# Moving blocks read as two halves in alternation, and PSUM read with a step of two, in a streaming-encoder layer

## The chip, the cores and the metric

The kernel runs on one core of one Trainium2 chip. Its metric is the device time of one execution in microseconds; the program is launched once and holds the whole layer. TensorE (PE) multiplies a stationary block of 128 columns, which it loads first (PEld), with a moving block of up to 512 columns and writes the products to PSUM. VectorE (DVE) and ScalarE (ACT) read PSUM; GpSimd (POOL) and SyncE (SP) start transfers.

## The reference, cut to what matters

```python
x = x + 0.5 * swiglu_ffn(rmsnorm(x, ffn1_norm), w_gate1, w_up1, w_down1)
x = x + hybrid_mixer(rmsnorm(x, mix_norm), w_in, q_norm, k_norm, rel_bias, pool_w, pool_scale, w_out)
x = x + 0.5 * swiglu_ffn(rmsnorm(x, ffn2_norm), w_gate2, w_up2, w_down2)
return rmsnorm(x, final_norm)

def swiglu_ffn(x, w_gate, w_up, w_down):
    return (silu(x @ w_gate) * (x @ w_up)) @ w_down
```

x has 512 tokens of 1024 features, the feed-forward width is 2816, all in float32. The mixer projects to q, k, v (512 columns each, 8 heads of 64) and u (512 columns). Attention is in chunks of 64 over the own and the 8 previous chunks, with normalised q and k and a learned bias. u goes through trailing means over 2, 4, 8 and 16 tokens, less the token itself, a 128x128 map and a scale for each of four groups. Both results, side by side, go through `w_out`.

## The kernel before, in words

**A product of high and low parts.** Each float32 operand is split in a high part (ScalarE's cast to float32r) and the remainder (VectorE). `mm3` makes one product of two such pairs as three matmuls into one PSUM bank: high x high (L188), high x low (L189), low x high (L190). Each matmul loads its own stationary block. Every large product of the kernel goes through `mm3`.

**The stages.** First comes the norm of x and the up stage of the first feed-forward layer (gate and up projections). The first feature blocks (5 in the first layer, 4 in the second, "plain") are multiplied as they are, with all 512 tokens as the moving block; meanwhile VectorE and ScalarE prepare sums and differences of token halves and feature halves (`blocks`). The other 17 and 18 blocks are multiplied in a scheme with seven products in place of eight: a unit for one block has 7 x 4 calls of `mm3` with moving blocks of 256 tokens. In a unit the order on PE, DVE and ACT is written out by hand. ScalarE copies some of the results out of PSUM (`copy`, L561) or takes their silu (L626), and VectorE adds others (L605, L619), multiplies gate and up (`place`, L717) and makes sums and remainders of the next unit's weights (L472, L490, L496, L497).

The down stage uses the same scheme of seven products (`Down`). The first layer has weights as the stationary and 256 tokens as the moving block; the second has tokens as the stationary and 512 (in part 256) weight columns as the moving block. `gain` and `shared` (first layer), `residual` and a list of additions (second) bring the results into x.

The mixer lies between the layers. Its steps are jobs with an engine, a cost and a rank, and `plan` puts them in order: it simulates the engines with these costs. The cost of one `mm3` is the constant `T_MM3`. Projections on PE fill in wherever nothing of higher rank is ready. The jobs' buffers and their places in PSUM come out of the same plan. Weight transfers of the mixer are jobs on SP (L1101), with a cast on ScalarE (L1106) and a remainder on VectorE (L1111). The norm's steps on TensorE are four products of one column with `ones` (L1140; L309 in the up stages) and a product of 512 columns in full float32 (L1171; L330 in the up stages). Transposes of q and k are at L1344. Scores, transposes of the probabilities and the products with v (L1501, L1565, L1590) call TensorE directly, without `mm3`.

**Where operands lie.** High and low parts of the weights lie in `parts_sb` at offsets that are given by hand, in the unit loop with a shift of 16 columns (`SHIFT`).

Of the kernel before, what the change touches and what calls it, by code (L numbers as in the profile page):

```python
# [12 lines left out]
ALU = mybir.AluOpType  # L13
# [34 lines left out]
)  # L48
HOP = 0.45
SLOW = dict(act=1.06, dve=1.06)  # L50
T_MM3 = 0.685
MIX_ENGINES = {
    mybir.EngineType.PE, mybir.EngineType.DVE, mybir.EngineType.Activation, mybir.EngineType.Pool,
}
# [2 lines left out]
def layer(  # L57
# [117 lines left out]
    def weights(src, parts=1):  # L175
# [6 lines left out]
            split(raw[:, part], hi[:, part], lo[:, part])  # L182
        return hi, lo

    def mm3(acc, a, b, start, stop, further=False):

        more = dict(skip_group_check=True) if further else {}
        nc.tensor.matmul(acc, a[0], b[0], start=start, stop=False, **more)  # L188
        nc.tensor.matmul(acc, a[0], b[1], start=False, stop=False, **more)  # L189
        nc.tensor.matmul(acc, a[1], b[0], start=False, stop=stop, **more)  # L190

    def cut(pair, lo, n):
        return pair[0][:, lo : lo + n], pair[1][:, lo : lo + n]
# [208 lines left out]
    def ffn_up(norm, wA, down, loaded, in_order, plain, turns=()):  # L402
# [8 lines left out]

        def evacuate(f, gate, up):
            g = temp()
            nc.vector.tensor_tensor(g, gate, norm.rb, op=ALU.mult)
            sg = temp()
            nc.scalar.activation(sg, g, AF.Silu)

            nc.vector.tensor_tensor(sg, sg, norm.rb, op=ALU.mult)
            down.place(f, up, sg)
            down.sums(f)  # L420
            return sg

# [135 lines left out]
                )  # L558

        def copy(dst, src, scale=1.0):  # L560
            nc.scalar.activation(dst, src, AF.Copy, scale=scale)  # L561

        def nothing():
            pass
# [4 lines left out]
        with tc.manual_schedule(engines={E.PE, E.DVE, E.Activation}):  # L569
            last_silu = last_place = last_sums = nothing  # L570
            for n in range(plain, KF):
                f = down.order[n]
                acc, up_lo, up_hi = bank()[:, :HT], bank()[:, :HT], abank()[:, :HT]
                u, z, sg = temp(), temp(), temp()
                w11, w13, w24 = (w[n, i][:2] for i in (11, 13, 24))
                if n == KF - 1:
                    down.load(new_sum())
                    down.load(new_sum())
                product(acc, w11, A11, True)
                ends = n == KF - 1  # L580
# [12 lines left out]
                low11(n + 1)  # L593
                if ends:
                    down.first_tokens(0)
                last_sums()
                sum13(n + 1)
                copy(z[:, HT:], up_hi, -1.0)
                product(acc, cut(w24, 0, S), S2, False)
                copy(u[:, HT:], acc, -1.0)  # L600
                sum24(n + 1)
                if ends:
                    down.first_tokens(1)
                product(up_hi, cut(w24, S, S), A22, False)
                nc.vector.tensor_tensor(u[:, HT:], up_hi, u[:, HT:], op=ALU.add)  # L605
                down.make_sums(u[:, HT:])
                if ends:
                    down.first_weights(0)
                product(acc, cut(w13, 0, S), S1, False)
                copy(z[:, :HT], acc)  # L610
                nc.vector.tensor_tensor(z[:, HT:], z[:, :HT], z[:, HT:], op=ALU.add)
# [7 lines left out]
                nc.vector.tensor_tensor(u[:, :HT], up_lo, u[:, :HT], op=ALU.add)  # L619
                low24(n + 1)  # L620
                if ends:
                    down.first_weights(1)
                product(acc, cut(w22, 0, S), S4, False)

                def last_silu(acc=acc, sg=sg):
                    nc.scalar.activation(sg[:, :HT], acc, AF.Silu, scale=-1.0)  # L626

                def last_place(f=f, u=u, sg=sg):
                    down.place(f, u, sg)
# [16 lines left out]
    class Down:  # L646
# [65 lines left out]
        def place(self, f, up, sg):  # L712
            k, second = self.pair(f)
            z = self.acts[k // 2][:, :, k % 2, :]
            up, sg = (y.rearrange("p (a c) -> p a c", a=2) for y in (up, sg))
            at = z[:, A12 : A22 + 1] if second else z[:, A11 : S3 + 1 : S3 - A11]
            nc.vector.tensor_tensor(at, up, sg, op=ALU.mult)  # L717

        def sums(self, f):

# [132 lines left out]
    with tc.tile_pool(name="act1", bufs=1, reuse_waits="tile") as apool, ExitStack() as in_order:  # L853
# [20 lines left out]

        def gain(i, d, t, acc, scale):
            z = whole_of(i, d, t)
            scaled(z, acc[i][0][0].rearrange("p (a c) -> p a c", a=2), scale, z)

        def shared(i, d, t, op):
            z = whole_of(i, d, t)  # L880
            nc.vector.tensor_tensor(z, z, u2[i].rearrange("p (a c) -> p a c", a=2), op=op)

        down1.product(p7, 0, S3, T3)
        for i in range(2):
# [45 lines left out]
    with tc.tile_pool(name="mix", bufs=1, reuse_waits="tile") as mpool:  # L930
# [366 lines left out]
        def project_qk(half, first):  # L1297
            var = {}

            def evacuate(t):  # L1300
                return lambda: nc.scalar.activation(
                    buf["q", half, t], buf[half, t], AF.Copy, scale=n2.r[:, t : t + 1]
                )

            def square(t):
# [74 lines left out]
        def project_v(first):  # L1380
            def finished(t, unit):
                def pair():
                    if v[t] is None:
                        v[t] = mpool.tile([P, NH, 2, HD], F32R, tag=f"v{t}", name=f"v{t}")
                    return v[t][:, :, 0, :], v[t][:, :, 1, :]

                high, low = scaled_pair(
                    lambda: buf["v", t].rearrange("p (h c) -> p h c", c=HD), pair,
                    lambda: n2.r[:, t : t + 1],
                )  # L1390
                z = job("act", 0.65, RANK["evac"], high, [unit, at_r])
# [6 lines left out]
        def project_u(g, first):  # L1398
# [8 lines left out]
            def evacuate():  # L1407
                u = buf["uu", g]
                nc.gpsimd.memset(u[:, :PAD], 0.0)
                nc.vector.tensor_tensor(u[:, PAD:], buf["u", g], n2.rb, op=ALU.mult)  # L1410

            def sums():
                s, step, n = buf["uu", g], 1, 0
# [33 lines left out]
            for k in range(KD):  # L1447
# [10 lines left out]
            z = job("dve", 0.62, rank, low, [z], uses=[("dd", g)])  # L1458
            z = job("pe", 0.71, RANK["map"], mapped, [z, at_wp], [("bank", ("map", g))], pair)
            high, low = scaled_pair(  # L1460
                lambda: buf["map", g], lambda: (buf["pT", g, 0], buf["pT", g, 1]),
                lambda: ps_sb[:, g : g + 1],
            )
            z = job("act", 0.65, rank, high, [z], [("m", ("pT", g, n)) for n in range(2)])
# [187 lines left out]

        def add_out(d):
            def emit():
                nc.vector.tensor_tensor(x[d], x[d], buf["out", d], op=ALU.add)

            return emit

# [90 lines left out]
    with tc.tile_pool(name="act2", bufs=1, reuse_waits="tile") as apool, ExitStack() as in_order:  # L1749
# [21 lines left out]
        def residual(half, t, acc, lo=0, n=S, scale=0.5):  # L1771

            z = xt[half * NT + t][:, lo : lo + n]
            nc.vector.scalar_tensor_tensor(z, acc[:, :n], scale, z, op0=ALU.mult, op1=ALU.add)

        def settle(half, t, part, lo=0, n=S):

# [56 lines left out]
        for tt in range(2):  # L1834
            scaled(u2[tt], p1[tt][0][0], 0.5, u2[tt], ALU.subtract)
            residual(1, 2 + tt, p5[tt][0][0])
            for i in (2 + tt, NT + tt, NT + 2 + tt):
                op = ALU.subtract if i < NT + 2 else ALU.add
                todo.append((nc.vector.tensor_tensor, xt[i], xt[i], u2[tt], op))
        for g in range(G):  # L1840
            if g + 1 < G:
                down2.product(p7, g + 1, S3, T3)
# [154 lines left out]
```

## Time and profile before

| what | value |
|---|---|
| time, median of 3 runs | 830.56 us (830.5 to 831.28) |
| span of the profiled execution, first to last instruction | 828.4 us |
| DVE busy in the span | 713.3 us, 86% |
| ACT busy | 500.3 us, 60% |
| POOL busy | 147.2 us, 18% |
| moved by DMA | 158.56 MB, 191 GB/s on average |

The profiled execution has no time of its own beside its span; the median of the runs stands 2.2 us above that span. [...] In lists of groups, `x8 | 3.3, 417` means eight instructions, 3.3 us busy in all, 417 ns each. On the line of a window the numbers with counts are the busy times of PE, PEld, DVE, ACT and POOL in this order, then the granted clock, the share of the DMA engines and GB/s.

### The profile page before, as it was taken

What the parts mean: (1) busy time and instruction counts of PE and PEld (TensorE: products, weight loads), DVE (VectorE), ACT (ScalarE), POOL (GpSimd) and SP (SyncE); (2) the same over time, 40 slices, a digit from 0 to 9 for tenths busy, and PEclk for the clock granted to TensorE, in tenths of its full rate; (3) what the DMA queues carried; (4) which work ended last, traced back from release to release, by engine and by line L of the source; (5) the groups of instructions that cost most, each with busy time, mean ns of one, the idle gap of its engine ahead of it and who ended that gap; (6) DMA issues with size and microseconds to landing.
All of it is one profiled execution on the core that took longest, in us unless ns stands there. A gap on an engine that the chain in (4) does not pass through costs nothing.

```text
span 828.4 us, 15013 instructions
## 1 busy us (share of the span) xinstructions
PE 819.0 (99%) x5730; PEld 754.3 (91%) x5730; DVE 713.3 (86%) x1123; ACT 500.3 (60%) x854; POOL 147.2 (18%) x234
## 2 busy tenths in 40 slices
PE   9999999999999999999999999999999999999996
PEld 7889999999999999888878888899999999988885
DVE  7899999899996987677688689988999999977896
ACT  8346555666766665559659544455665556756573
POOL 0013212222310000100265372111111011100010
PEclk9999999999999999999999999999999999999998
DMA  8276889879998674430599867255766475959632
GB/s 287 69 204 206 239 221 255 210 201 232 252 301 280 217 214 140 142 100 30 167 242 237 251 146 213 64 125 193 156 185 157 150 213 147 276 195 319 201 115 102
DMA packets 73703, 158.56 MB, mean 191 GB/s; under 512 B 6544, under 2 KB 31648, under 8 KB 73248
## 3 DMA queue, kind: packets, MB, share of 16 engines
q1 hardware_dynamic: 49664, 109.09, 39.3%
q0 software_dynamic: 23680, 48.24, 27.9%
q8 instruction: 45, 0.74, 0.4%
q10 hardware_dynamic: 288, 0.27, 0.1%
q14 instruction: 26, 0.21, 0.1%
HBM read 153.38 MB, written 50.34 MB: 246 GB/s over the span
## 4 chain that ended last, share of the span: by engine, by line
PE 98%; DVE 1%; ACT 0%; DMA 0%; issue 0%; DVEq 0%
PE mm L188 21%; PE mm L190 21%; PE mm L189 21%; PE a L188 10%; PE a L190 10%; PE a L189 10%; PE a L1590 1%; PE mm L1501 1%; PE a L1565 1%; PE mm L1565 0%; PE mm L1590 0%; DMA gain_sb<-in_gains_dram 0%; PE a L1501 0%; PE mm L1344 0%; PE a L309 0%; PE a L330 0%
## 5 line engine op out<-in xcount | busy, mean ns | idle before, releaser
L561 ACT ACTIVATE t<-mm 128x256 f32<-128x256 f32 x105 | 40.4, 385 | 115.2 <-PE mm L190 112.5
L132 ACT CAST parts<-raw 128x1024 fp32r<-128x1024 f32 (+2 forms) x77 | 74.2, 970 | 58.6 <-PE mm L189 24.2
L133 DVE TENSOR_TENSOR parts<-raw,parts 128x1024 fp32r<-128x1024 f32 (+2 forms) x77 | 85.7, 1121 | 16.8 <-ACT parts L132 16.3
L188 PE MATMUL mm<-ha,parts 128*128 128x256 f32 x280 | 77.3, 276 | 0.0
L190 PE MATMUL mm<-ha,parts 128*128 128x256 f32 x280 | 77.3, 276 | 0.0
L189 PE MATMUL mm<-ha,parts 128*128 128x256 f32 x280 | 77.3, 276 | 0.0
L707 POOL DMA_DIRECT2D wsum<-in_wB_dram x72 | 71.4, 1135 | 26.2 <-DMA wsum<-wsum 14.2
L705 POOL COPY mark<-t 128x1 f32<-128x1 f32 x40 | 16.0, 401 | 337.5 <-DVE t L605 249.6
L472 DVE TENSOR_TENSOR parts<-wsum,parts 128x1024 fp32r<-128x1024 f32 x53 | 64.6, 1219 | 5.8 <-PE mm L190 4.5
L467 ACT CAST parts<-wsum 128x1024 fp32r<-128x1024 f32 x53 | 53.9, 1048 | 0.3
L188 PEld LDWEIGHTS mm<-ha,parts 128*128 128x128 f32 x280 | 52.6, 188 | 0.1
L189 PEld LDWEIGHTS mm<-ha,parts 128*128 128x128 f32 x280 | 52.6, 188 | 0.1
L190 PEld LDWEIGHTS mm<-ha,parts 128*128 128x128 f32 x280 | 52.6, 188 | 0.0
L133 DVE TENSOR_TENSOR ah<-acts,ah 128x512 fp32r<-128x512 f32 (+1 forms) x72 | 47.2, 663 | 5.6 <-ACT ah L132 5.6
L188 PE MATMUL mm<-hhi,parts 128*128 128x512 f32 x128 | 50.2, 396 | 0.3 <-ACT parts L132 0.3
L190 PE MATMUL mm<-hhi,parts 128*128 128x512 f32 x128 | 50.0, 394 | 0.0
L189 PE MATMUL mm<-hlo,parts 128*128 128x512 f32 x128 | 49.8, 391 | 0.0
L132 ACT CAST ah<-acts 128x512 fp32r<-128x512 f32 (+1 forms) x72 | 40.9, 580 | 10.5 <-PE mm L189 7.5
L472 DVE TENSOR_TENSOR parts<-raw,parts 128x512 fp32r<-128x512 f32 (+1 forms) x52 | 43.4, 858 | 0.0
L490 DVE TENSOR_TENSOR wsum<-raw 128x1024 f32<-128x1024 f32 x35 | 42.6, 1217 | 0.0
L467 ACT CAST parts<-raw 128x512 fp32r<-128x512 f32 (+1 forms) x52 | 39.3, 755 | 2.2 <-DMA raw<-in_wA_dram 1.5
L188 PE MATMUL mm<-xa,parts 128*128 128x256 f32 x140 | 38.8, 277 | 0.0
(340 smaller groups left out, 3044.5 us busy)
## 6 DMA issues: line engine op xcount, KB each, us to landing
raw<-in_wA_dram SPq DMA_DIRECT2D x87, 512.0 KB, 5.0
wsum<-in_wB_dram POOLq DMA_DIRECT2D x60, 512.0 KB, 7.0
raw<-wsum SPq DMA_DIRECT2D x36, 512.0 KB, 4.8
raw<-in_wB_dram SPq DMA_DIRECT2D x30, 512.0 KB, 5.0
wsum<-wsum POOLq DMA_DIRECT2D x20, 512.0 KB, 5.3
x<-in_xT_dram SPq DMA_DIRECT2D x16, 256.0 KB, 6.2
raw<-in_wQK_dram SPq DMA_DIRECT2D x8, 512.0 KB, 3.5
wsum<-in_wB_dram POOLq DMA_DIRECT2D x12, 256.0 KB, 5.5
```

Of the source, the lines that this page charges most:

```text
L132: nc.scalar.copy(hi, src)
L133: nc.vector.tensor_tensor(lo, src, hi.bitcast(F32), op=ALU.subtract)
L188: nc.tensor.matmul(acc, a[0], b[0], start=start, stop=False, **more)
L189: nc.tensor.matmul(acc, a[0], b[1], start=False, stop=False, **more)
L190: nc.tensor.matmul(acc, a[1], b[0], start=False, stop=stop, **more)
L467: nc.scalar.copy(hi, src)
L472: nc.vector.tensor_tensor(lo, src, hi.bitcast(F32), op=ALU.subtract)
L490: nc.vector.tensor_tensor(z, raw[:, : 2 * S], raw[:, S : 3 * S], op=ALU.add)
L561: nc.scalar.activation(dst, src, AF.Copy, scale=scale)
L705: nc.gpsimd.tensor_copy(mark[:, 0:1], after[:, 0:1])
L707: nc.gpsimd.dma_start(self.rows(i, g), self.rows(self.terms[i][at], g), **(dict(accum_op=ALU.add) if at else {}),)
L1501: nc.tensor.matmul(spot(h, t), q[a][rows, t * P : (t + 1) * P], k[b][rows, : (t + 1) * P], start=a + b == 0, stop=a == 1,)
```

## The change

Every `mm3` now reads the moving block's two halves in alternation: column 0 of the first half, column 0 of the second, column 1 of the first, and so on. The stationary blocks and the number of matmuls stay the same, and PSUM is still written from the first column to the last; it now holds the two halves interleaved. Each reader of such a bank on VectorE and ScalarE reads every second column for the first half and then every second column for the second (`ordered`), and writes two contiguous runs (`natural`). Where the halved share is copied out as it lies, its later readers in SBUF have the step.

In `gain` an instruction over 2 x 256 columns becomes two over 256. The planner's cost of one `mm3` goes from 0.685 to 0.655 us.

```diff
-T_MM3 = 0.685
+T_MM3 = 0.655
...
+    def ordered(acc):
+        return acc.rearrange("p (i a) -> p a i", a=2)
+
+    def natural(z):
+        return z.rearrange("p (a i) -> p a i", a=2)
+
     def mm3(acc, a, b, start, stop, further=False):
         more = dict(skip_group_check=True) if further else {}
-        nc.tensor.matmul(acc, a[0], b[0], start=start, stop=False, **more)
-        nc.tensor.matmul(acc, a[0], b[1], start=False, stop=False, **more)
-        nc.tensor.matmul(acc, a[1], b[0], start=False, stop=stop, **more)
+        acc = acc.rearrange("p (i a) -> p i a", a=2)
+        high, low = (z.rearrange("p (a i) -> p i a", a=2) for z in b)
+        nc.tensor.matmul(acc, a[0], high, start=start, stop=False, **more)
+        nc.tensor.matmul(acc, a[0], low, start=False, stop=False, **more)
+        nc.tensor.matmul(acc, a[1], high, start=False, stop=stop, **more)
...
-            nc.vector.tensor_tensor(g, gate, norm.rb, op=ALU.mult)
+            nc.vector.tensor_tensor(natural(g), ordered(gate), natural(norm.rb), op=ALU.mult)
...
-            down.place(f, up, sg)
+            down.place(f, ordered(up), sg)
...
-            nc.scalar.activation(dst, src, AF.Copy, scale=scale)
+            nc.scalar.activation(natural(dst), ordered(src), AF.Copy, scale=scale)
...
-                nc.vector.tensor_tensor(u[:, HT:], up_hi, u[:, HT:], op=ALU.add)
+                nc.vector.tensor_tensor(natural(u[:, HT:]), ordered(up_hi), natural(u[:, HT:]), op=ALU.add)
...
         def gain(i, d, t, acc, scale):
             z = whole_of(i, d, t)
-            scaled(z, acc[i][0][0].rearrange("p (a c) -> p a c", a=2), scale, z)
+            for f in range(2):
+                part = acc[i][0][0][:, f * HT : (f + 1) * HT]
+                scaled(natural(z[:, f]), ordered(part), scale, natural(z[:, f]))
 
         def shared(i, d, t, op):
-            z = whole_of(i, d, t)
-            nc.vector.tensor_tensor(z, z, u2[i].rearrange("p (a c) -> p a c", a=2), op=op)
+            z = whole_of(i, d, t).rearrange("p f (a i) -> p f a i", a=2)
+            nc.vector.tensor_tensor(z, z, u2[i].rearrange("p (f i a) -> p f a i", f=2, a=2), op=op)
...
         def residual(half, t, acc, lo=0, n=S, scale=0.5):
             z = xt[half * NT + t][:, lo : lo + n]
-            nc.vector.scalar_tensor_tensor(z, acc[:, :n], scale, z, op0=ALU.mult, op1=ALU.add)
+            nc.vector.scalar_tensor_tensor(
+                natural(z), ordered(acc[:, :n]), scale, natural(z), op0=ALU.mult, op1=ALU.add
+            )
```

The readers in the mixer (q and k, v, u, the pooling map, the output projection) and the other two of the unit loop change in the same way.

The order of the up and down stages on TensorE stays row for row the same. In the mixer the planner's new number moves rows. TensorE at the start of the mixer, where `mm` are the banks of the q and k projection, `parts` its weights and `hhi`, `hlo` the normalised tokens; before:

```order
L188 MATMUL mm_4280<-parts,hhi_4224 128x512
L189 MATMUL mm_4280<-parts,hhi_4224 128x512
L190 MATMUL mm_4280<-parts,hlo_4225 128x512
L1140 MATMUL a_4355<-ones,acc_4117 128x1 x4
L188 MATMUL mm_4286<-parts,hhi_4224 128x512
L189 MATMUL mm_4286<-parts,hhi_4224 128x512
L190 MATMUL mm_4286<-parts,hlo_4225 128x512
```

Of the change, the same place on TensorE:

```order
L198 MATMUL mm_4290<-parts,hhi_4234 128x512
L199 MATMUL mm_4290<-parts,hhi_4234 128x512
L200 MATMUL mm_4290<-parts,hlo_4235 128x512
L198 MATMUL mm_4296<-parts,hhi_4234 128x512
L199 MATMUL mm_4296<-parts,hhi_4234 128x512
L200 MATMUL mm_4296<-parts,hlo_4235 128x512
L1151 MATMUL a_4366<-ones,acc_4125 128x1 x4
```

The norm's sums (L1140, now L1151) stand behind one `mm3` more; the product with the diagonal (L1171) moves likewise. VectorE at the end of the first down stage, where `x` are the residual tiles and `a` the banks of the last product; before:

```order
L1111 TENSOR_TENSOR parts<-raw_4260,parts 128x1024
L1111 TENSOR_TENSOR parts<-raw_4262,parts 128x1024
L822 SCALAR_TENSOR_TENSOR x_2854<-a_3414,x_2854 128x2x256
L1111 TENSOR_TENSOR parts<-raw_4284,parts 128x1024
L822 SCALAR_TENSOR_TENSOR x_2855<-a_3415,x_2855 128x2x256
L136 SCALAR_TENSOR_TENSOR hlo_4225<-x_2854,gain_sb,hhi_4224 128x512
```

Of the change, the same place on VectorE:

```order
L1122 TENSOR_TENSOR parts<-raw_4270,parts 128x1024
L1122 TENSOR_TENSOR parts<-raw_4272,parts 128x1024
L831 SCALAR_TENSOR_TENSOR x_2854<-a_3414,x_2854 128x256 x2
L831 SCALAR_TENSOR_TENSOR x_2855<-a_3415,x_2855 128x256 x2
L136 SCALAR_TENSOR_TENSOR hlo_4235<-x_2854,gain_sb,hhi_4234 128x512
```

The two gains are two instructions each, and the remainder of a mixer weight (L1111) no longer stands between them. On SP, weight transfers (L1101) at the same part of the program; before:

```order
L1101 DMA raw_4290<-in_wQK_dram 128x1024
L1101 DMA raw_4337<-in_wV_dram 128x1024
L1192 DMA t_4264<-ext_d 32x2x256 x4
L1192 DMA t_4269<-ext_d 32x2x256 x4
L1244 DMA t_4277<-in_wP_dram 128x512
```

Of the change, the same place on SP:

```order
L1112 DMA raw_4300<-in_wQK_dram 128x1024
L1203 DMA t_4274<-ext_d 32x2x256 x4
L1203 DMA t_4279<-ext_d 32x2x256 x4
L1255 DMA t_4287<-in_wP_dram 128x512
L1112 DMA raw_4347<-in_wV_dram 128x1024
```

The first transfer of the v weights stands behind those of the bias and of the pooling map.

More of the change, by code (lines that the diff above doesn't have):

```diff
@@ L618, in ffn_up @@
                 nc.scalar.activation(sg[:, HT:], z[:, HT:], AF.Silu)
-                nc.vector.tensor_tensor(u[:, :HT], up_lo, u[:, :HT], op=ALU.add)
+                nc.vector.tensor_tensor(natural(u[:, :HT]), ordered(up_lo), natural(u[:, :HT]), op=ALU.add)
                 low24(n + 1)
@@ L625, in last_silu @@
                 def last_silu(acc=acc, sg=sg):
-                    nc.scalar.activation(sg[:, :HT], acc, AF.Silu, scale=-1.0)
+                    nc.scalar.activation(natural(sg[:, :HT]), ordered(acc), AF.Silu, scale=-1.0)
                 def last_place(f=f, u=u, sg=sg):
-                    down.place(f, u, sg)
+                    down.place(f, natural(u), sg)
                 def last_sums(f=f):
@@ L714, in place @@
             z = self.acts[k // 2][:, :, k % 2, :]
-            up, sg = (y.rearrange("p (a c) -> p a c", a=2) for y in (up, sg))
             at = z[:, A12 : A22 + 1] if second else z[:, A11 : S3 + 1 : S3 - A11]
-            nc.vector.tensor_tensor(at, up, sg, op=ALU.mult)
+            nc.vector.tensor_tensor(at, up, natural(sg), op=ALU.mult)
         def sums(self, f):
@@ L1301, in evacuate @@
                 return lambda: nc.scalar.activation(
-                    buf["q", half, t], buf[half, t], AF.Copy, scale=n2.r[:, t : t + 1]
+                    natural(buf["q", half, t]), ordered(buf[half, t]), AF.Copy,
+                    scale=n2.r[:, t : t + 1],
                 )
@@ L1384, in pair @@
                         v[t] = mpool.tile([P, NH, 2, HD], F32R, tag=f"v{t}", name=f"v{t}")
-                    return v[t][:, :, 0, :], v[t][:, :, 1, :]
+                    return [v[t][:, :, i, :].rearrange("p (a h) c -> p a h c", a=2) for i in range(2)]
                 high, low = scaled_pair(
-                    lambda: buf["v", t].rearrange("p (h c) -> p h c", c=HD), pair,
+                    lambda: buf["v", t].rearrange("p (h c a) -> p a h c", a=2, c=HD), pair,
                     lambda: n2.r[:, t : t + 1],
@@ L1409, in evacuate @@
                 nc.gpsimd.memset(u[:, :PAD], 0.0)
-                nc.vector.tensor_tensor(u[:, PAD:], buf["u", g], n2.rb, op=ALU.mult)
+                nc.vector.tensor_tensor(
+                    natural(u[:, PAD:]), ordered(buf["u", g]), natural(n2.rb), op=ALU.mult
+                )
             def sums():
@@ L1460, in project_u @@
             high, low = scaled_pair(
-                lambda: buf["map", g], lambda: (buf["pT", g, 0], buf["pT", g, 1]),
+                lambda: ordered(buf["map", g]),
+                lambda: (natural(buf["pT", g, 0]), natural(buf["pT", g, 1])),
                 lambda: ps_sb[:, g : g + 1],
@@ L1654, in emit @@
             def emit():
-                nc.vector.tensor_tensor(x[d], x[d], buf["out", d], op=ALU.add)
+                nc.vector.tensor_tensor(natural(x[d]), natural(x[d]), ordered(buf["out", d]), op=ALU.add)
             return emit
@@ L1773, in residual @@
             z = xt[half * NT + t][:, lo : lo + n]
-            nc.vector.scalar_tensor_tensor(z, acc[:, :n], scale, z, op0=ALU.mult, op1=ALU.add)
+            nc.vector.scalar_tensor_tensor(
+                natural(z), ordered(acc[:, :n]), scale, natural(z), op0=ALU.mult, op1=ALU.add
+            )
         def settle(half, t, part, lo=0, n=S):
@@ L1838, in layer @@
                 op = ALU.subtract if i < NT + 2 else ALU.add
-                todo.append((nc.vector.tensor_tensor, xt[i], xt[i], u2[tt], op))
+                z = natural(xt[i])
+                todo.append((nc.vector.tensor_tensor, z, z, ordered(u2[tt]), op))
         for g in range(G):
```

## The prediction

> **What bounds the kernel now.** I read the page's busy times and its chain first, then who waited for whom, then single products on the timeline. The first fence is from the page.
>
> ```profile
> span 828.4 us, 15013 instructions
> ...
> PE 819.0 (99%) x5730; PEld 754.3 (91%) x5730; DVE 713.3 (86%) x1123; ACT 500.3 (60%) x854; POOL 147.2 (18%) x234
> ...
> PEclk9999999999999999999999999999999999999998
> ...
> PE 98%; DVE 1%; ACT 0%; DMA 0%; issue 0%; DVEq 0%
> ```
>
> TensorE is busy for 819.0 of 828.4 us, its clock is granted in full, and 98% of the chain that ended last is TensorE. The list of waits, asked for TensorE alone, has two entries:
>
> ```profile
> PE a L224 <- DVE eps L214: 1.1, 1, 1.1
> PE mm L188 <- ACT parts L132: 0.3, 1, 0.3
> ```
>
> So nothing makes TensorE wait; what counts is how long one product occupies it. The durations in the profile (276 ns for 256 columns) are latencies that overlap, so I take the distance between starts. Timeline of 180 to 200 us (256 columns) and of 730 to 744 us (512 columns), first and last row of each:
>
> ```profile
> 179.80 0.28 PE L188 MATMUL mm<-xa,parts 128*128 128x256 f32 x1
> ...
> 199.97 0.28 PE L189 MATMUL a<-ha,parts 128*128 128x256 f32 x1
> 729.84 0.39 PE L190 MATMUL mm<-parts,ah 128*128 128x512 f32 x1
> ...
> 743.89 0.39 PE L189 MATMUL mm<-parts,ah 128*128 128x512 f32 x1
> ```
>
> The first pair holds 179 rows: 20.17 us over 178 steps, 113.3 ns each. The second holds 63 rows: 14.05 us over 62 steps, 226.6 ns. Twice the columns take exactly twice the time, 0.4426 ns a column, with no fixed part. Two other rows show columns without the products' rate: the full-precision product at L330 (two passes of 512 columns) and the transposes at L1344 (128 columns).
>
> ```profile
> 26.66 1.02 PE L330 MATMUL a<-t,ones 128*128 128x512 f32 x2
> 27.11 0.79 PE L189 MATMUL mm<-hlo,whi 128*128 128x512 f32 x1
> 27.74 0.39 PE L190 MATMUL mm<-hhi,wlo 128*128 128x512 f32 x1
> ...
> 362.57 1.91 PE L1344 MATMUL mm<-ident,t 128*128 128x128 f32 x16
> ...
> 364.55 0.40 PE L189 MATMUL a<-parts,hhi 128*128 128x512 f32 x1
> ```
>
> A pass at L330 takes (27.74 - 26.66 - 0.227) / 2 = 0.427 us, a transpose (364.55 - 362.57 - 0.227) / 16 = 0.1096 us. Between 128 and 512 columns that is 0.827 ns a column and 3.8 ns fixed. Half of 0.827 is 0.413: the products run at nearly twice that column rate, but each column costs 0.4426, a surcharge of 7% per column (about one column's time in every fifteen or sixteen), while the fixed part has vanished behind it. Something that feeds columns falls short at the full rate and is sufficient at half of it.
>
> **The products.** There are 3996 products of 256 columns: 3 for each of (17 + 18) x 28 in the two up stages, 308 in the first down stage and 44 on half banks in the second. There are 1416 of 512 columns: 3 x (144 plain up + 196 mixer + 132 down). At 113.3 and 226.6 ns they make 452.7 + 320.9 = 773.6 us of the 828.4. In the changed kernel each half of a moving block is asked for one column in two steps, which is the column rate at which L330 shows no surcharge. I take it that the surcharge goes, and the fixed part shows again: 512 x 0.4133 + 3.8 = 215.4 ns, and 256 x 0.4133 + 3.8 = 109.6 ns. No row of before has alternating columns, so the bounds are a saving of all of it and a loss (rivals below).
>
> What is late next on TensorE is the weight load. Products of one column show it (timelines of PE and of PEld):
>
> ```profile
> 340.31 0.95 PE L1140 MATMUL a<-ones,acc 128*128 128x1 f32 x8
> 341.08 0.19 PEld L188 LDWEIGHTS mm<-parts,hhi 128*128 128x128 f32 x1
> ```
>
> The load for the second of the eight starts with the first at 340.31, and the load behind the eighth at 341.08: seven loads in 0.77 us, 0.110 each, up to 0.112 by the rounding. I take 0.111. It binds the 256-column products (109.6 is below it) and not those of 512.
>
> Saving: 3996 x (113.3 - 111.0) = 9.2 us, and 1416 x (226.6 - 215.4) = 15.9 us; 25.1 us together. If loads don't bind, the first is 3996 x 3.7 = 14.8 and the sum 30.7 us.
>
> [...]
>
> **The readers of PSUM.** VectorE and ScalarE now read columns two apart and write two runs. Rows of before, VectorE (groups by form, 140 to 220 us and 30 to 60 us; then the windows):
>
> ```profile
> L611 DVE TENSOR_TENSOR t<-t 128x256 f32<-128x256 f32 x8 | 3.4, 420 | 2.5 <-ACT t L561 2.5
> L619 DVE TENSOR_TENSOR t<-mm,t 128x256 f32<-128x256 f32 x8 | 3.3, 418 | 0.0
> L605 DVE TENSOR_TENSOR t<-a,t 128x256 f32<-128x256 f32 x8 | 3.3, 417 | 0.0
> ...
> L414 DVE TENSOR_TENSOR t<-mm,rb 128x512 f32<-128x512 f32 x3 | 2.0, 679 | 0.0
> ...
> 100.00:220.00 120.00, 120.00 (x1061) 120.00 (x1060) 110.26 (x155) 71.29 (x129) 27.75 (x40) 1.00 0.89 220
> ...
> 30.00:60.00 30.00, 30.00 (x134) 24.82 (x134) 29.73 (x41) 12.70 (x17) 5.76 (x6) 1.00 0.46 128
> ...
> 340.00:500.00 160.00, 160.00 (x833) 132.31 (x832) 122.27 (x278) 105.56 (x209) 53.21 (x78) 1.00 0.61 165
> ```
>
> The columns after the length are the busy time of PE, PEld, DVE, ACT and POOL, the clock, the DMA share and GB/s. A read from PSUM (417) costs what one from SBUF does (420), and (679 - 417) / 256 = 1.02 ns a column. VectorE works at one column a nanosecond, less than half of the rate at which TensorE fills the bank, so I take no extra for the step. The ends are nothing and one more column time, 1.02 ns, for each column read. No row shows a gain, and I allow none. The twelve additions of the halved shares in the two down stages now read SBUF with that step; they wait in a list for a free place on VectorE, and I charge them nothing (at most 12 x 0.52 = 6 us of VectorE).
>
> In the up stage VectorE is busy for 110.26 of 120 us, 8.1% spare, and TensorE shortens by 2.0%: covered. At 30 to 60 us, in the plain blocks and the preparation of the token blocks, it is busy for 29.73 of 30. TensorE would shorten these 30 us by 11.2 / 226.6, 1.5 us, and VectorE has 0.3 to give: 1.2 us of the saving is lost there, and by the same stage of the second layer about 0.3. I charge 1.5 us. ScalarE, 71.29 of 120, has room for any of its ends.
>
> In `gain` a read of 512 columns (it goes through L822) becomes two of 256:
>
> ```profile
> L822 DVE SCALAR_TENSOR_TENSOR x<-mm,x x6: 679/680/692, 268.9 to 315.0; 128x512 f32<-128x512 f32 x6
> ...
> L822 DVE SCALAR_TENSOR_TENSOR x<-a,x x4: 682/688/692, 294.2 to 330.2; 128x512 f32<-128x512 f32 x4
> ```
>
> 2 x 417 - 680 = 154 ns more, ten times, 1.5 us of VectorE between 269 and 331 us. The last four stand before the mixer's normalisation, while TensorE has products of the projections to do, so I cost them nothing; without that cover they would be 0.6 us.
>
> The planner's number moves mixer steps by a few places: on TensorE the products at L1140 and L1171 stand behind three more projection products each (0.7 us a time), and on SP one weight transfer goes behind two bias transfers and the pool weights, with its cast on ScalarE and remainder on VectorE. TensorE waits for none of this before, because projection products fill in beside each chain, and VectorE is busy for 122.27 of the mixer's 160 us. I cost it nothing, with 2 us either way as the bound, three such delays of 0.7 us. The transfers get no more room in a shorter kernel:
>
> ```profile
> 240.00:250.00 10.00, 10.00 (x91) 10.00 (x90) 9.44 (x13) 8.18 (x12) 1.14 (x1) 1.00 1.14 302
> ...
> 750.00:760.00 10.00, 10.00 (x46) 8.27 (x45) 5.95 (x10) 6.66 (x11) 0.00 (x0) 1.00 0.98 380
> ```
>
> The fullest stretch of the first down stage moves 302 GB/s with TensorE never waiting, and 380 are reached elsewhere, so 2% more rate is there; nothing charged.
>
> Sum: 830.56 - 25.1 + 1.5 = 807 us. The sum is made on the profiled execution, whose span of 828.4 stands 2.2 us below the median of the runs; I keep these 2.2 as they are, since launch and end are not touched.
>
> **Rivals.** *Loads don't bind.* The loads of 0.110 were seen with products of one column, where product and load may add; then 830.6 - 30.7 + 1.5 = 801 us.
>
> *The step costs VectorE a second column time.* Then L605 and L619 add 0.52 us to each unit of 84 products. The unit lasts 84 x 113.3 = 9.52 us, shrinks to 9.32, and VectorE's 8.75 in it grows to 9.27: just held. The nine plain blocks add 2 x 0.52 each, 9.4 us where it is full, and the mixer's evacuations about 1: 817 us. For it speaks that no row has such a read, against it that VectorE's columns are slow already.
>
> *Half of the surcharge stays.* 818 us.
>
> *The change does nothing.* If the pause belongs to the bytes fetched and not to their order, the same bytes bring the same pauses, for alternation touches as many: 830 to 833 us, the top with the step on VectorE.
>
> *Weight load and moving block collide* (slower). At the end of the kernel 256-column products are further apart:
>
> ```profile
> 817.21 0.28 PE L190 MATMUL a<-whi,ah 128*128 128x256 f32 x1
> ...
> 820.09 0.28 PE L190 MATMUL a<-parts,ah 128*128 128x256 f32 x1
> ```
>
> 25 rows, 24 steps of 120.0 ns: 6.7 more than in the rows above for the same size. Line, engine and shape are the same and only the tiles' places differ, so where operands lie can cost 6.7 ns. The tiles of before lie so that it is rare; alternation reads two places at once. If all products paid it on top of the lower rate, 256 columns would take 116.3 and 512 columns 222.1 ns: 3996 x 3.0 - 1416 x 4.5 = +5.6 us, 836 us. With s the share that pays, the saving of 25.1 falls by s x (3996 x 5.3 + 1416 x 6.7) = 30.7 s, so it decides from s = 0.8.
>
> *A column that does not follow its neighbour halves the rate* (slower). At L330's pace 256 columns take 213 and 512 take 427 ns: 3996 x 0.100 + 1416 x 0.200 = +683 us, 1514 us. Any pause above 7% a column is a loss. [...] No run here shows strided columns yet; against it the trace has only that half rate is free of pauses.
>
> **How the numbers follow.** Loads bind 0.45 (807); they don't 0.20 (801); VectorE's step 0.10 (817); half stays 0.05 (818); nothing 0.08 (831, of which 0.05 within 0.2% and 0.03 above, by the extra work on VectorE); collisions 0.06 (836); half rate 0.06 (1514). The first four are the faster ones, 0.80. Less than 0.2% (1.7 us), about what a measurement of this kernel can tell, counts as the same: 0.05. Slower: 0.15. The range takes the first four with their bounds: below, 801 less 2 for the mixer and 2 for the fixed part; above, 818 plus 2 for the mixer and 2 for gains without cover: 797 to 822. The likeliest alone is 803 to 811.
>
> **What would show it.** Right: starts 111 ns apart for 256 columns and 215 for 512; L605's and L414's successors at 417 and 679 ns; TensorE still over 97% of the chain, and its waits under 3 us, at 30 to 66 us. Wrong: 109 or 113 ns for 256 columns; VectorE reads over 0.6 us for 256 columns; distances that differ by tile; TensorE waiting for remainders (L133) in the up stages.

## The result, and the profile after

The changed kernel takes 811.97 us (median of 4 runs, 811.67 to 812.59) against 830.64 us before on the same chip: 0.9776 of the time, 95% interval 0.9763 to 0.979. The profiled execution took 811.69 us with a span of 809.7. The forecast was 807.0 us, range 797 to 822.

The page after, in the order in which the lines of before were read:

```profile
span 809.7 us, 14959 instructions
...
PE 797.8 (99%) x5730; PEld 749.1 (93%) x5730; DVE 712.8 (88%) x1133; ACT 498.8 (62%) x854; POOL 147.2 (18%) x234
...
PEclk9999999999999999999999999999999999999998
...
PE 91%; DVE 4%; ACT 1%; issue 1%; DVEq 0%; ACTq 0%
```

TensorE is still what sets the time, but no longer alone: its part of the chain that ended last fell from 98% to 91%, and VectorE's rose to 4%. The clock is as before (0.997 of full, granted on average in both). The time went out of single products. Timelines of TensorE, first and last row of three stretches: 256 columns at 180 to 200 us, 512 columns at 712 to 726 us, and the last 256-column products of the kernel:

```profile
179.75 0.28 PE L199 MATMUL mm<-ha,whi 128*128 128x256 f32 x1
...
199.96 0.28 PE L200 MATMUL mm<-ha,parts 128*128 128x256 f32 x1
711.80 0.38 PE L198 MATMUL mm<-parts,ah 128*128 128x512 f32 x1
...
725.83 0.38 PE L200 MATMUL a<-parts,ah 128*128 128x512 f32 x1
798.01 0.27 PE L198 MATMUL a<-whi,ah 128*128 128x256 f32 x1
...
801.25 0.28 PE L200 MATMUL a<-parts,ah 128*128 128x256 f32 x1
```

The first pair holds 182 rows, 20.21 us over 181 steps: 111.7 ns each (113.3 before). The second holds 66 rows, 14.03 us over 65 steps: 215.8 ns (226.6 before). The third holds 30 rows, 3.24 us over 29 steps: 111.7 ns, where before they were 120.0.

The instructions of VectorE that read PSUM with the step (groups by form, 140 to 215 us, and that of the plain blocks and of `gain` over the whole span; busy us, mean ns of one):

```profile
L615 DVE TENSOR_TENSOR t<-a,t 128x256 f32<-128x256 f32 x8 | 3.3, 418 | 0.0
L629 DVE TENSOR_TENSOR t<-mm,t 128x256 f32<-128x256 f32 x8 | 3.3, 418 | 0.0
...
L424 DVE TENSOR_TENSOR t<-mm,rb 128x512 f32<-128x512 f32 x9 | 6.1, 682 | 2.1 <-ACT rb L342 2.1
...
L831 DVE SCALAR_TENSOR_TENSOR x<-a,x 128x256 f32<-128x256 f32 x8 | 3.0, 420 | 2.5 <-PE a L200 2.5
```

417 and 418 became 418, 679 became 682: the step of two costs VectorE nothing. ScalarE's copies out of PSUM (L561, now L571) take 385 ns before and after. What TensorE waits for now, and the three windows of before (same columns):

```profile
PE a L234 <- DVE eps L224: 1.1, 1, 1.1
PE mm L200 <- DVE parts L133: 0.8, 1, 0.8
PE mm L198 <- DVE m L1621: 0.6, 1, 0.6
PE a L319 <- DVE acc L315: 0.4, 1, 0.4
PE a L1605 <- DVE pTw L1594: 0.3, 1, 0.3
```

```profile
30.00:60.00 30.00, 29.23 (x136) 25.29 (x135) 29.96 (x41) 12.85 (x17) 5.76 (x6) 1.00 0.46 132
100.00:220.00 120.00, 120.00 (x1077) 120.00 (x1076) 112.12 (x158) 72.24 (x130) 28.23 (x41) 1.00 0.90 225
340.00:500.00 160.00, 159.00 (x852) 136.34 (x851) 127.88 (x286) 106.79 (x211) 56.08 (x83) 1.00 0.64 175
```

The up stage (100 to 220 us) is as covered as forecast: VectorE went from 110.26 to 112.12 of 120 us and TensorE waits for nothing. At 30 to 60 us VectorE is full (29.96 of 30 us) and TensorE has lost 0.77 us, all of it here:

```profile
51.10 1.22 DVE L133 TENSOR_TENSOR parts<-raw,parts 128x1024 fp32r<-128x1024 f32 x1
...
52.37 0.70 PE L200 MATMUL mm<-hhi,parts 128*128 128x512 f32 x2 [0.77 <-DVE parts L133]
```

In the mixer TensorE waits a full microsecond that it did not wait before. The next section says which line of the diff that is.

### The profile page after: what moved, and what is told of

Same layout as the page of the kernel before. It is cut to its first block, busy times and chain, and to the rows that moved or that the text cites. A ratio compares the mean times of both kernels' runs of the same rounds, so it can differ in the third digit from the quotient of the medians.

```text
span 809.7 us, 14959 instructions
## 1 busy us (share of the span) xinstructions
PE 797.8 (99%) x5730; PEld 749.1 (93%) x5730; DVE 712.8 (88%) x1133; ACT 498.8 (62%) x854; POOL 147.2 (18%) x234
## 4 chain that ended last, share of the span: by engine, by line
PE 91%; DVE 4%; ACT 1%; issue 1%; DVEq 0%; ACTq 0%
PE mm L198 19%; PE mm L200 19%; PE mm L199 19%; PE a L199 10%; PE a L200 9%; PE a L198 9%; PE mm L1605 1%; PE mm L1516 1%; DVE aside L365 1%; PE a L1580 1%; PE mm L1580 1%; DVE aside L371 0%; PE a L1516 0%; DVE parts L133 0%; PE a L1605 0%
## 5 line engine op out<-in xcount | busy, mean ns | idle before, releaser
L571 ACT ACTIVATE t<-mm 128x256 f32<-128x256 f32 x105 | 40.5, 386 | 110.8 <-PE mm L200 108.8
L133 DVE TENSOR_TENSOR parts<-raw,parts 128x1024 fp32r<-128x1024 f32 (+2 forms) x77 | 85.8, 1121 | 15.1 <-ACT parts L132 14.7
L200 PE MATMUL mm<-ha,parts 128*128 128x256 f32 x280 | 77.0, 275 | 0.0
L198 PE MATMUL mm<-ha,parts 128*128 128x256 f32 x280 | 77.0, 275 | 0.0
L715 POOL COPY mark<-t 128x1 f32<-128x1 f32 x40 | 15.9, 397 | 330.9 <-DVE t L615 244.8
L198 PEld LDWEIGHTS mm<-ha,parts 128*128 128x128 f32 x280 | 53.8, 192 | 0.1
L199 PEld LDWEIGHTS mm<-ha,parts 128*128 128x128 f32 x280 | 53.8, 192 | 0.1
L200 PEld LDWEIGHTS mm<-ha,parts 128*128 128x128 f32 x280 | 53.8, 192 | 0.0
L198 PE MATMUL mm<-hhi,parts 128*128 128x512 f32 x128 | 49.6, 391 | 0.2
L200 PE MATMUL mm<-hhi,parts 128*128 128x512 f32 x128 | 48.7, 384 | 0.8 <-DVE parts L133 0.8
L133 DVE TENSOR_TENSOR ah<-acts,ah 128x512 fp32r<-128x512 f32 (+1 forms) x72 | 47.1, 662 | 2.7 <-ACT ah L132 2.4
L1122 DVE TENSOR_TENSOR parts<-raw,parts 128x1024 fp32r<-128x1024 f32 x24 | 30.1, 1258 | 11.6 <-ACT parts L1117 11.5
```

The costliest lines, as they stand in the source:

```text
L133: nc.vector.tensor_tensor(lo, src, hi.bitcast(F32), op=ALU.subtract)
L198: nc.tensor.matmul(acc, a[0], high, start=start, stop=False, **more)
L199: nc.tensor.matmul(acc, a[0], low, start=False, stop=False, **more)
L200: nc.tensor.matmul(acc, a[1], high, start=False, stop=stop, **more)
L571: nc.scalar.activation(natural(dst), ordered(src), AF.Copy, scale=scale)
L1122: nc.vector.tensor_tensor(lo, buf["raw", i], hi.bitcast(F32), op=ALU.subtract)
```

## The experiments

**Which part of the change does what.** The theory: all of the gain comes from the order of columns in the products, with a saving for each column that is the same for both sizes except where loads bind; the readers and the planner's number are worth less than 1 us. The rivals: the readers' step costs something that the gain hides, or the planner's new order helps or hurts by more.

e1_old_number is the changed kernel with the planner's old number:

```diff
-T_MM3 = 0.655
+T_MM3 = 0.685
```

> The changed kernel with the planner's number back at 0.685. Theory (the saving is the products' column rate, the mixer's order is worth next to nothing): 811 to 813 us, products 111.7 and 215.8 ns apart. Rival (the new order of the mixer cost the microsecond by which the mixer saved less than its products did): 810 to 811 us. Rival (the new number is part of the gain): 814 us or more.

Measured: 810.48 us (809.7 to 811.88), ratio 0.9754, interval 0.9741 to 0.9767: 1.5 us faster than with the new number, and the fastest of the versions that leave nothing out. The intervals of the two ratios overlap, so the mirror image decides.

e2_number_alone is the kernel before with nothing but the new number:

```diff
-T_MM3 = 0.685
+T_MM3 = 0.655
```

> The kernel before with the planner's number at 0.655 and nothing else. Theory: within 1 us of 830.6, products 113.3 and 226.7 ns apart. Rival (the order is part of the gain): 828 us or less.

Measured: 832.47 us (831.91 to 833.1) against 830.89, ratio 1.002, interval 1.0011 to 1.0029: 1.6 us slower. The number costs the same 1.5 us with and without alternation, and "less than 1 us" was wrong for it. The place shows in the window 400 to 460 us (attention), here in the order before, e2, after, e1 (the column behind the length is TensorE's busy time):

```profile
400.00:460.00 60.00, 60.00 (x323) 49.43 (x323) 49.62 (x125) 42.90 (x92) 32.16 (x42) 1.00 0.82 218
```

```profile
400.00:460.00 60.00, 59.10 (x328) 48.81 (x328) 48.36 (x123) 42.10 (x93) 30.15 (x41) 1.00 0.78 214
```

```profile
400.00:460.00 60.00, 58.99 (x332) 50.66 (x331) 52.43 (x127) 44.92 (x95) 31.79 (x43) 1.00 0.86 214
```

```profile
400.00:460.00 60.00, 59.70 (x335) 51.27 (x334) 50.35 (x125) 44.65 (x94) 32.87 (x43) 1.00 0.88 226
```

With 0.685 TensorE idles for nothing (before) and 0.30 us (e1), with 0.655 for 0.90 and 1.01. In the list of waits these are the entries for `m` (L1621, the attention result's remainder) and `pTw` (L1594), which before and e1 do not have. The place of most of it is the mixer: the changed kernel and e1 start its first products together (324.36 and 324.37 us) and the first product behind it, of the second up stage, 1.03 us apart (488.09 and 487.06). The rest of the 1.5 us is not named by a wait.

e3_readers_alone is the changed kernel with the products' order of before; the readers, the split of `gain` and the number stay:

```diff
-        acc = acc.rearrange("p (i a) -> p i a", a=2)
-        high, low = (z.rearrange("p (a i) -> p i a", a=2) for z in b)
+        high, low = b
```

> The changed kernel with the products' moving blocks and PSUM writes in the old order: only the readers with the step, the split gain and the new number remain. It leaves the columns of each product in another order than its readers expect, so its output is not the reference's. Theory (a read with a step of two costs VectorE and ScalarE nothing): 830 to 832 us, 417 ns for 256 columns and 679 for 512 as before. Rival (the readers cost something that the faster products hid): 833 us or more.

Measured: 832.54 us (832.36 to 833.33), ratio 1.002, interval 1.0011 to 1.0029. That is e2's time within 0.1 us. Readers and split are free; the number is all that e3 pays.

e4_512_alone alternates only in products of 512 columns:

```diff
-        acc = acc.rearrange("p (i a) -> p i a", a=2)
-        high, low = (z.rearrange("p (a i) -> p i a", a=2) for z in b)
+        high, low = b
+        if acc.shape[-1] == S:
+            acc = acc.rearrange("p (i a) -> p i a", a=2)
+            high, low = (z.rearrange("p (a i) -> p i a", a=2) for z in b)
```

> The changed kernel with alternation in the products of 512 columns alone; those of 256 read in the old order, so their columns land in another order than the readers expect. Theory (surcharge per column, weight load as the floor at 256): 1416 products save 10.8 ns each, 15.3 us, less about 2 us of waits in the plain blocks and the mixer: 817 to 819 us, 256-column products still 113.3 ns apart. Rival (a saving per product, whatever its size): a quarter of 18.7 us, about 826 us.

Measured: 819.4 us (818.66 to 819.87), ratio 0.9857, interval 0.9842 to 0.9872. Between e4 and the changed kernel lie 7.4 us, for the 256-column products; between e3 and e4 lie 13.1 us, for those of 512. The latter is 2.2 below the 15.3 that the distances give (1416 x 10.84 ns). TensorE's waits are of that size: L133 and L319 wait for 0.8 and 0.4 us in e4 and not at all in e3, and the wait shown here takes 1.5 us in e4, 0.4 in e3 and nothing in the changed kernel, so it is also part of the 7.4:

```profile
PE mm L200 <- ACT parts L132: 1.5, 1, 1.5
```

So the saving is not one for each product: it is 10.8 ns at 512 columns and 1.7 at 256. Nor is it one for each column alone, which would be 5.4 at 256: something else binds there.

**Why alternation is faster.** The prediction's reason was that each half is asked for one column in two steps, half the column rate. Any alternation that asks each half at half the rate on average should then do as well. The rival: what counts is that neighbours are not asked for in successive steps, so that any order without adjacent columns would do. Four kernels change only the order in which the products take the columns; PSUM is still written from the first column to the last, the readers are those of the changed kernel, and each had one run beside the kernel before at 830.92 us.

e5_step2 takes every second column, and then the others (0, 2, 4, ... 1, 3, 5, ...); e6_run4 and e7_run16 take runs of 4 and 16 columns from the halves in turn; e8_four takes four quarters in turn:

```diff
-        acc = acc.rearrange("p (i a) -> p i a", a=2)
-        high, low = (z.rearrange("p (a i) -> p i a", a=2) for z in b)
+        acc = acc.rearrange("p (a i) -> p a i", a=2)                           # e5
+        high, low = (z.rearrange("p (i a) -> p a i", a=2) for z in b)
...
+        acc = acc.rearrange("p (i a r) -> p i a r", a=2, r=4)                  # e6; e7 with r=16
+        high, low = (z.rearrange("p (a i r) -> p i a r", a=2, r=4) for z in b)
...
+        acc = acc.rearrange("p (i a) -> p i a", a=4)                           # e8
+        high, low = (z.rearrange("p (a i) -> p i a", a=4) for z in b)
```

> The changed kernel, whose products read every second column of the whole block and then the others, so one place is read at a time and successive columns are 8 bytes apart; columns land in another order than the readers expect. Theory (each half is asked at half the rate): one place is still asked at the full rate, over twice the bytes, so the surcharge stays or doubles: 113 to 120 ns for 256 columns, 227 to 240 for 512, 830 to 880 us. Rival (the pause belongs to columns that lie next to each other): 111.7 and 215.8 ns, 812 us.

> The changed kernel, whose products alternate between the halves in runs of 4 columns (16 bytes); columns land in another order than the readers expect. Theory (each half is asked at half the rate, on the average of a few columns): 111.7 and 215.8 ns, 812 us. Rival (adjacent columns cause the pause): three of four neighbours are adjacent again, so most of the surcharge returns: 224 ns for 512 columns, 113 for 256, 826 us.

> The changed kernel, whose products alternate in runs of 16 columns (64 bytes, the length of which one in seventeen column times was the surcharge); columns land in another order than the readers expect. Theory: if what falls short has room for 16 columns, 111.7 and 215.8 ns and 812 us; if not, the surcharge is back, 113.3 and 226.7 ns, 832 us. Rival (adjacent columns): 226 ns, 831 us.

> The changed kernel, whose products go round four quarters of the moving block, one column each; columns land in another order than the readers expect. Theory: each quarter is asked at a quarter of the rate, no surcharge: 111.7 and 215.8 ns, 812 us. Rival (more places at once cost more): over 226.7 ns for 512 columns.

Measured: 1606.99, 916.15, 874.82 and 1014.83 us. Products of 512 columns on their timelines, first and last row of a stretch of each (e5, e6, e7, e8):

```profile
1399.56 0.63 PE L200 MATMUL mm<-parts,ah 128*128 128x512 f32 x1
...
1414.97 0.64 PE L198 MATMUL mm<-parts,ah 128*128 128x512 f32 x1
```

```profile
799.73 0.42 PE L199 MATMUL a<-wlo,ah 128*128 128x512 f32 x1
...
814.98 0.41 PE L200 MATMUL mm<-parts,ah 128*128 128x512 f32 x1
```

```profile
764.81 0.40 PE L199 MATMUL a<-wlo,ah 128*128 128x512 f32 x1
...
779.93 0.40 PE L199 MATMUL a<-parts,ah 128*128 128x512 f32 x1
```

```profile
899.73 0.45 PE L198 MATMUL mm<-whi,ah 128*128 128x512 f32 x1
...
914.74 0.45 PE L200 MATMUL mm<-whi,ah 128*128 128x512 f32 x1
```

With 35, 62, 64 and 54 rows these are 453, 250, 240 and 283 ns a product, against 227 in contiguous order and 216 in alternation. Both theories fall. Half the rate for each half is not enough (e6 to e8 have it or less), and not asking for neighbours in succession is no help either (e5 is twice as slow).

**A second theory: two streams.** Write each order as two lists, the columns asked in even steps and those asked in odd steps. In alternation each list runs through one half in steps of one column (4 bytes): 216 ns. In contiguous order each list runs in steps of two columns (8 bytes): 227 ns. In e5 each runs in steps of four (16 bytes): 453 ns. In e6, e7 and e8 both lists jump between distant places: 240 to 283 ns. So the theory says that the fetch serves even and odd steps apart, and each wants the neighbour of the column that it fetched last. The rival: the two places must lie far apart, as the halves do. e9_near4 and e10_near16 tell these apart, with the two lists 4 and 16 columns away from each other (e9: 0, 4, 1, 5, 2, 6, 3, 7, 8, 12, ...):

```diff
-        acc = acc.rearrange("p (i a) -> p i a", a=2)
-        high, low = (z.rearrange("p (a i) -> p i a", a=2) for z in b)
+        acc = acc.rearrange("p (k i a) -> p k i a", a=2, i=4)                  # e10 with i=16
+        high, low = (z.rearrange("p (k a i) -> p k i a", a=2, i=4) for z in b)
```

> The changed kernel, whose products alternate between neighbouring pieces of 4 columns (columns 0, 4, 1, 5, 2, 6, 3, 7, then 8, 12 and so on); columns land in another order than the readers expect. Theory (the odd and the even steps of a moving block are two streams, and each is free of pauses if it takes columns that lie next to each other; contiguous order gives each a step of 8 bytes and 226.7 ns, halves in alternation 4 bytes and 215.8, every second column 16 bytes and 451): both streams have 4 neighbours in a row, so 215.8 to 220 ns for 512 columns, 111.7 to 113 for 256, 812 to 820 us. Rival (the two places must lie far apart): 226 ns or more, 830 us or more.

> The changed kernel, whose products alternate between neighbouring pieces of 16 columns (64 bytes); columns land in another order than the readers expect. Theory (two streams): each takes 16 neighbours in a row, 215.8 ns for 512 columns and 111.7 for 256, 812 us. Rival (one pause wherever a stream leaves a piece of 64 bytes by a jump): 226 to 240 ns, 830 to 875 us. If 4 columns are slower than 16, a jump itself costs.

Measured: 811.73 and 811.44 us, one run each. Timelines of e9 and of e10, 712 to 726 us, 67 rows each:

```profile
711.74 0.38 PE L198 MATMUL mm<-parts,ah 128*128 128x512 f32 x1
...
725.99 0.38 PE L198 MATMUL a<-parts,ah 128*128 128x512 f32 x1
```

```profile
711.75 0.38 PE L199 MATMUL mm<-parts,ah 128*128 128x512 f32 x1
...
725.99 0.38 PE L199 MATMUL a<-parts,ah 128*128 128x512 f32 x1
```

14.25 and 14.24 us over 66 steps, 216 ns: the full gain with streams 16 and 64 bytes apart. Distance falls; the theory separates the orders that gain from those that lose, among all eight that were timed. That the memory works in two such streams is inferred from times alone. It does not give the sizes among those that lose: both streams of e8 jump at every step and take 283 ns, while those of e5 move on by 16 bytes and take 453. Nor does any run tell it from another rule with two places open at a time, in which even and odd steps do not matter.

**What limits 256 columns.** The theory is the weight load of 128 columns. The rival is a floor of the product itself. e11_load64 halves the load in one of the three products, for 256 columns only, and leaves out half of that product's rows:

```diff
-        nc.tensor.matmul(acc, a[0], low, start=False, stop=False, **more)
+        m = P // 2 if 2 * acc.shape[1] == HT else P
+        nc.tensor.matmul(acc[:m], a[0][:, :m], low, start=False, stop=False, **more)
```

> The changed kernel, in which the second of the three matmuls of each 256-column product loads 64 stationary columns in place of 128 and leaves out half of that product's rows. Theory (the weight load is the floor for 256 columns): the matmul that loads 64 starts 109.2 ns after the one before it, the two that load 128 stay at 111.7; 3.3 us less in all, 808 to 809.5 us. Rival (111.7 is the product's own time at 256 columns): all stay at 111.7, 812 us.

Measured: 808.6 us, one run; the changed kernel's is 811.97. Its timeline at 180 to 200 us, first and last of 183 rows:

```profile
179.77 0.27 PE L200 MATMUL mm<-ha,whi 128*64 128x256 f32 x1
...
199.94 0.28 PE L198 MATMUL mm<-ha,parts 128*128 128x256 f32 x1
```

20.17 us over 182 steps, 110.8 ns on average. If one distance in three is shorter and two stay at 111.67, the short one is 3 x 110.82 - 2 x 111.67 = 109.1 ns, and 1332 x 2.5 = 3.3 us is what the time shows. A product of 256 columns can be followed after 109.1 ns.

The expectation names no row for its 109.2 ns; the changed kernel's trace has 109 or 110 ns behind 20 of its products of 256 columns. The short step does not lie where the expectation put it. The trace keeps starts to 1 ns; on average over the 256-column products of the whole kernel the step from the first matmul to the one that loads 64 (L198 to L200) takes 111.8 ns, the step behind that one (L200 to L201) 109.1, and the third 111.7. In the short step 128 columns are loaded, in the first only 64. So the theory foretold the wrong step, and the rival, by which no step is shorter, falls too. The edit halves both the load and the product's own stationary columns, so it does not tell which of them counts. For the load speaks L1140 in the kernel before: its one-column products, which load 128 columns each, start 111.7 ns apart from the second to the eighth (670 ns over six steps), as the 256-column products do after. Against it speak the transposes of L1344, which load 128 columns each and start 109.1 ns apart. What makes the floor of 111.67 ns stays open.

The floor explains 2.5 of the 3.7 ns by which 256 columns fall short of the 5.4. The other 1.2 are, by an estimate from the two distances, half of a fixed part of 2.5 ns that both sizes pay in alternation (2 x 109.14 - 215.83).

**Can VectorE's full stretch be relieved?** e12_pool_mult is e1 with one multiplication of each plain block on GpSimd:

```diff
-            nc.vector.tensor_tensor(sg, sg, norm.rb, op=ALU.mult)
+            nc.gpsimd.tensor_tensor(sg, sg, norm.rb, op=ALU.mult)
```

> The changed kernel with the planner's number at 0.685, and in the plain blocks the multiplication of the silu by the norm's factor on GpSimd in place of VectorE. Theory (VectorE, full from 30 to 60 us, now delays TensorE by about 1 us there): 0.5 to 1.3 us less than the 810.5 us of that number alone, no wait of TensorE for a remainder at 51 us. Rival (the wait moves to the later GpSimd result, or the two engines delay each other): 810.5 us or more.

Measured: 820.46 us (817.98 to 821.41), ratio 0.9868, interval 0.9847 to 0.9889, 10 us slower than e1. TensorE's waits, VectorE's wait for the multiplications, these on GpSimd (groups of its line), and what ScalarE waited for ahead of the longest stall:

```profile
PE a L198 <- ACT t L571: 3.1, 2, 2.9
PE mm L198 <- DVE acts L726: 2.1, 1, 2.1
PE mm L200 <- DVE parts L133: 1.3, 2, 1.1
PE mm L198 <- ACT t L571: 1.1, 1, 1.1
```

```profile
DVE acts L726 <- POOL t L428: 4.3, 4, 1.2
```

```profile
L428 POOL TENSOR_TENSOR t<-t,rb 128x512 f32<-128x512 f32 x9 | 20.2, 2244 | 74.7 <-ACT t L426 69.4 <-DMA raw<-in_wA_dram 5.3
```

```profile
79.43 0.62 ACT L477 CAST parts<-raw 128x512 fp32r<-128x512 f32 x1 [4.08 <-DMA raw<-in_wA_dram]
```

One multiplication takes 2244 ns on average, three times VectorE's 681. VectorE waits for it at L726, 4.3 us in all, and TensorE for L726 2.1 us, so the wait moved to the later GpSimd result, as the rival had it; the wait for remainders (L133) grew from 0.8 to 1.3 us. Ahead of the longest stall ScalarE waited 4.08 us for a weight transfer. SyncE starts that transfer, at 69.6 us, and it lands after 9.8; e1 starts it at 66.5 and has it after 6.6. Why it came late was not shown. The stretch was not relieved, and what relief there would bring stays open.

## Why the prediction was right, and where it was off

The direction, the place and the size hold: 18.7 us saved of a forecast 23.6. The missing 4.9 us by its own terms:

- *512 columns, 15.9 us.* Measured 226.67 to 215.83 ns, 1416 x 10.84 = 15.3 us, 0.6 less. The surcharge per column goes and, by the estimate above, a fixed part returns, as forecast (2.5 ns, forecast 3.8).
- *256 columns, 9.2 us.* That a floor binds them, and not the column rate, is right (e11 has steps of 109.1 ns), but it is 111.67 ns, not 111.0: 3996 x 1.67 = 6.7 us, 2.5 less. The price came from seven loads timed to 0.01 us, 0.110 to 0.112; over 3996 products that rounding alone spans 8 us, and the text took a value inside it without carrying its width. That the floor is the weight load was argued and is not shown (e11).
- *The planner's number, nothing within 2 us.* It costs 1.5 us (e1, e2), inside the bound. "Projection products fill in beside each chain" failed in attention, where TensorE idles 0.9 to 1.0 us for `m` and `pTw`.
- *VectorE full at 30 to 60 us, 1.5 us lost.* The trace has the 0.77 us shown and shorter gaps of some 0.1 to 0.3 us, together 1.4 us in the first layer and 0.5 in the second: 1.9 us, 0.4 more.
- *The readers of PSUM, nothing; `gain`, nothing.* Both held (418, 682 and 420 ns; e3).

These are 0.6 + 2.5 + 1.5 + 0.4 = 5.0 us of the 4.9, but that the sum closes so well is luck. It takes the distances of the stretches shown for all products, and some stood wider apart before. Over the whole trace, steps without a stall (under 125 and 245 ns from start to start) average 113.54 and 227.64 ns before and 111.65 and 215.87 after. By these the products give 7.5 + 16.7 = 24.2 us, near the forecast 25.1, and 5.5 us are lost to waits and longer steps, where 1.5 were charged. So the losses were sized worst; the planner's number and VectorE are 3.4 of the 5.5, a new wait of 0.4 us at L319 is another part, and the rest has no name here.

Of the signs that the prediction named, the starts near 111 and 215 ns and the durations of VectorE's reads came. The chain did not: 91% of it is TensorE, where over 97% was named, and TensorE's waits come to 3.2 us, not under 3. "TensorE waiting for remainders (L133) in the up stages" was named as a sign of being wrong, and it came, 0.77 us at 51 us; it is the loss that the prediction itself had charged for that stretch.

The reason behind the gain did not hold. "Something that feeds columns falls short at the full rate and is sufficient at half of it" would have promised the same gain to e6, e7 and e8, which lose 44 to 184 us. The row it rested on (L330, 427 ns a pass, twice 213.5 beside the 215.83 of alternation) was true, but it does not tell a lower rate from a better order. That the order which was chosen is one of the three that gain, among the eight timed, was luck, as far as that reason goes. The rivals "loads don't bind" (as a price: 109.6 ns), "VectorE's second column time", "half of the surcharge stays" and "the change does nothing" fall by the distances and durations above; so does "collide", since 256-column products 120 ns apart no longer occur. "Half rate" is what e5 shows: it was the right price, 1514 us forecast and 1607 measured, for another order.

## What to carry to other kernels

Where TensorE is busy all the time, compare the distance between starts with the column time that other rows give (here half of L330's 427 ns a pass, the author's estimate); a surcharge that grows with the columns (here 227 ns against 216 at 512 columns) may lie in how the moving block is fetched, and the order of columns can be chosen freely as long as the readers undo it. The times here went by how the columns of even steps and of odd steps follow each other, not by how successive columns do (216, 227 and 453 ns at 512 columns for steps of 4, 8 and 16 bytes). A cost that a planner uses is part of a change: time it by itself, since a truer number gave a worse plan here (1.5 us), and the old number with the new order is the version to keep (810.48 us).

## What the runs showed of the hardware

- Products of 512 float32r columns took 216, 227 and 453 ns as the columns of even and of odd steps each advanced by 4, 8 and 16 bytes (alternation, contiguous order, e5). The 216 came with the two places 16 bytes, 64 bytes or half a block apart (e9, e10, the changed kernel).
- The last 256-column products stood 120.0 ns apart before, 6.7 more than others of their size, and 111.7 in alternation. That the 6.7 ns come from where operands lie was inferred, not shown. Whether the shift of 16 columns between high and low parts is still needed was not tried.
- Products of 256 columns in alternation start 111.67 ns apart with 128 stationary columns, and the product behind one with 64 stationary columns starts after 109.1 (e11).
- After the stall of 2.9 us in e12 the granted clock fell to half, and products of 256 columns ran 213 ns apart (11 steps from 81.68 to 84.03 us) until 84.5 us. The timeline, and the window with its granted clock (last but two):

```profile
80.38 0.38 PE L198 MATMUL a<-ha,parts 128*128 128x256 f32 x1 [2.93 <-ACT t L571]
...
81.68 0.42 PE L198 MATMUL a<-ha,parts 128*128 128x256 f32 x1
...
84.03 0.42 PE L200 MATMUL mm<-ha,wlo 128*128 128x256 f32 x1
```

```profile
81.50:84.50 3.00, 3.00 (x16) 3.00 (x16) 2.92 (x5) 0.00 (x0) 0.00 (x0) 0.50 0.71 282
```

This stall cost its own length and about 1.6 us behind it (16 products, 0.1 us more each). The stall of 2.1 us at 528 us of the same run had no such stretch behind it: the granted clock over 500 to 540 us was 1.00. That the stall's length is what brings the clock down is not shown.
